# Later turns for streamed modulation sums, a later place for the gate sigmoids, and two accumulators in the first column group of a decoder layer

## The chip, the cores and the metric

The kernel runs on one core of a Trainium2 chip. The metric is the device time of one execution in microseconds; the value given for a kernel is the median of its runs. A profile shows one further execution, recorded instruction by instruction.

## What is computed

One layer of a hybrid decoder trunk, in fp32: batch 1, 256 positions, model width 2048. A vector `c` modulates both norms (adaLN); three token mixers share one input projection; a gated feed-forward part follows. Cut to what matters here:

```
mod = silu(c) @ w_ada + b_ada                       # 2048 -> 6 x 2048
shift1, scale1, gate1, shift2, scale2, gate2 = split(mod, 6)
h = rms_norm(x, norm1_gain) * (1 + scale1) + shift1  # 256 x 2048
proj = h @ w_in                                      # 2048 x 13840: q, k, v of three branches, r, gate columns
q, k of the dilated branch: rms_norm per head of 128
g = sigmoid(gate columns)                            # three branches x 2048
y = g0*(o_sb @ w_br_sb) + g1*(o_dil @ w_br_dil) + g2*(o_gla @ w_br_gla)
x = x + gate1 * (y @ w_out)
h = rms_norm(x, norm2_gain) * (1 + scale2) + shift2
x = x + gate2 * ((silu(h @ Wg) * (h @ Wu)) @ w_ffn_out)
```

## The kernel before

**Products.** Every large product keeps fp32 accuracy by splitting each operand into a high part that TensorE takes in its fast fp32 format and a low rest. A weight tile of 256 x 512 arrives in a buffer `raw` (four of them), ScalarE casts the high part `whi` (line 163), VectorE subtracts the low part `wlo` (line 164), and `mm3` issues three matmuls per row block and half of the positions (lines 171 to 173: high x high, high x low, low x high). A pair of row blocks with both halves of the positions is twelve weight matmuls. The low part frees `raw` for the next transfer; all transfers named here are issued by SyncE, in program order.

**The first projection in groups.** The modulated input H is needed transposed (channels on partitions), and shift and scale of its channels come out of `w_ada`. So that the projection need not wait for all of them, the 16 blocks of 128 channels are cut into five groups (0–2, 2–5, 5–8, 8–11, 11–16). The first four run over 16 column blocks of `w_in`, up and down in turn, and add into SBUF tiles `A`; a group's last block stays in its PSUM banks and is continued by the next group (`proj_block`, `carry`). The fifth takes its 16 blocks likewise, and after it come the blocks of `r` and the column blocks of the gates. While group g runs, the modulation columns of group g+1 are computed (`ada_group`): SyncE brings a piece of 128 rows of `w_ada` into one of six borrowed buffers (`T4`, `T5`, `OS0`–`OS2`, `OD`), VectorE multiplies it with silu(c) of those rows and adds it to an accumulator `ada` (`ada_mac`, lines 296 and 298), 16 steps to a sum; ADA_BY says by which block of the projection how many steps are issued. Then TensorE transposes the accumulator in columns of 128 (`turned_sums`, line 348), VectorE adds up along the row (line 349) and finishes shift and scale (lines 355, 358), and ScalarE and VectorE make H of the group (`make_h`, lines 466 to 473). There is one accumulator tile, so the next sum begins when the transposes of this one are done. The fifth group is summed in two pieces of two and of three channel blocks, each with shift and scale.

**The first group** has nothing to hide behind. `first_group` loads x and the pieces of `w_ada`, keeps TensorE at work with matmuls on constants (`keep_warm`, line 454; 22, 13 and 10 of them), transposes x with its norm factor (line 447; eight copies to `xT` by ScalarE, line 448), and sums 16 steps into one accumulator, the last in two halves. The column sums are single-column matmuls (`column_sum`, line 340).

**Order.** Each engine runs its instructions in a fixed order that a list scheduler decides when the program is built: by priority (`prio()` raises it by 4000, in the first group by 30000), by the tiles' readiness in its model, and by explicit edges (`tc.issue_after`). So an edit in one place can shift instructions of other parts, on all engines.

**After the groups.** The gate blocks (`gate_block`): each of the three gates has four column blocks of 512. Block 1 of each is among the 16 blocks of the groups (tiles `A13` to `A15`); block 0 is multiplied after the groups and its banks are copied as they are (line 1068). The sigmoids of these six tiles are taken in place (line 1086, tiles of 128 x 1024); the other column blocks take the sigmoid straight from the bank. In the same stretch run the norms of the dilated heads (`qk_norm`: squares on ScalarE at line 646, `rsqrt` with a logarithm and an exponential at lines 278 to 286, factors applied at line 654) and the transposes of the normed heads (`qk_turn`, line 666), the gated linear attention (lines 837 to 872), and the multiply-adds of the later modulation columns. Sigmoid, logarithm and exponential need other function tables on ScalarE; a switch is an instruction ACT_TABLE_LOAD, which stands under the line of the function that needs it.

Of the kernel before, what the change touches and what calls it, by code (L numbers as in the profile page):

```python
# [13 lines left out]
AF = mybir.ActivationFunctionType  # L14
# [64 lines left out]
def trunk(ctx: ExitStack, tc: tile.TileContext, I, out):  # L79
# [16 lines left out]
    def S(tag, shape, dtype=F32):  # L96
        return slot.tile(shape, dtype, tag=tag, name=nm(tag))
# [191 lines left out]

    w_ada = I["w_ada"]  # L290

    def ada_mac(acc, raw, k, zero=True):

        c = csil[:, k : k + 1]
        if k == 0 and zero:
            nc.vector.tensor_scalar(acc, raw, c, None, op0=ALU.mult)
        else:
            nc.vector.scalar_tensor_tensor(acc, raw, c, acc, op0=ALU.mult, op1=ALU.add)  # L298

    ADA_TAGS = ("T4", "T5", "OS0", "OS1", "OS2", "OD")  # L300

    mod1 = const.tile([P, 2, KC], F32, name="mod1")

    def ada_group(k0, k1, tags=ADA_TAGS, between=None):

        n = k1 - k0
        sh, sc = mod1[:, 0, k0:k1], mod1[:, 1, k0:k1]
        gains[GROUPS.index((k0, k1))] = (sh, sc)
        count = 0
        pieces = -(-n // 4)  # L310
        for i in range(pieces):
            a = k0 + n * i // pieces
            m = k0 + n * (i + 1) // pieces - a
            w = m * P
            acc = S("ada", [P, 2, w])
            for k in range(KC):
                with prio():
                    raw = S(tags[count % len(tags)], [P, 2, w])
                    nc.sync.dma_start(
                        raw,  # L320
                        w_ada[k * P : (k + 1) * P, : 2 * D].rearrange("p (s c) -> p s c", s=2)[:, :, a * P : a * P + w],
                    )
                    with tc.issue_after(state["macs_after"]) if "macs_after" in state else nullcontext():
                        ada_mac(acc, raw, k)
                count += 1
                if k < KC - 1:
                    yield
            if between is not None:
                between()
            with prio():  # L330
                c = slice(a - k0, a - k0 + m)
                sums = small([P, 2, m])
                for j in range(2):
                    turned_sums(sums[:, j, :], acc[:, j, :])
                finish_columns(sums[:, 0, :], sh[:, c], SEG_SHIFT1, a)
                finish_columns(sums[:, 1, :], sc[:, c], SEG_SCALE1, a, ROW_N1)
            yield

    def column_sum(ps, acc):
        return nc.tensor.matmul(ps, acc, ones[:, 0:1], start=True, stop=True)  # L340

    def turned_sums(dst, acc, behind=None):

        n = dst.shape[1]
        ps = misc_bank([P, n, P])
        for i in range(n):
            with tc.issue_after(behind) if behind is not None else nullcontext():
                nc.tensor.transpose(ps[:, i, :], acc[:, i * P : (i + 1) * P], ident)  # L348
        nc.vector.reduce_sum(dst, ps, axis=AX.X)

    def finish_columns(ps, dst, seg, k0, gain_row=None):

# [63 lines left out]
    def norm1():  # L416
# [22 lines left out]
        for t in range(NT):  # L439
            act(col(r, t), col(y, t), AF.Copy, scale=col(z, t))  # L440
            act(diag[:, t, :], ident, AF.Copy, scale=col(r, t))
        for j in range(4):
            for t in range(NT):
                ps = misc_bank([P, 4, P])
                for i in range(4):
                    xs = xin[2 * t + j // 2][:, j % 2, i * P : (i + 1) * P]
                    state["turn"] = nc.tensor.matmul(ps[:, i, :], xs, diag[:, t, :], start=True, stop=True)
                state["turned"] = nc.scalar.copy(xT[j][:, :, t * P : (t + 1) * P], ps)

    def keep_warm(n):  # L450

# [62 lines left out]
                else:  # L514
                    nc.vector.tensor_add(A[b][:, t, :], A[b][:, t, :], pss[t])  # L515

    gains = [None] * len(GROUPS)

    def h_group(g):
        k0, k1 = GROUPS[g]  # L520
        sh, sc = gains[g]
# [5 lines left out]
    def first_group():  # L527
# [21 lines left out]
        split = state["split"]  # L549
        load(range(5, KC // 2))  # L550
# [9 lines left out]
        acc = S("ada", [P, 2, w])  # L560
# [30 lines left out]
    def ada_groups():  # L591
        for a, b in GROUPS[1:]:
            yield from ada_group(a, b)

    nxt, done = ada_groups(), 0
    for g in range(LAST):
        base = ADA_BY[g - 1] if g else 0
        for n, b in enumerate(orders[g]):
            due = ADA_BY[0] * n // (GROUPED - 1) if g == 0 else base + (ADA_BY[g] - base) * (n + 1) // GROUPED
            while done < due and next(nxt, "end") != "end":  # L600
                done += 1
            if (g, n) == (0, 6):
                state.pop("casts_after", None)
                state.pop("macs_after", None)
            proj_block(g, b, early if (g, n) == (0, 0) else None, carry=n == GROUPED - 1)
        if g == LAST - 1:
            for _ in nxt:
                pass
        h_group(g + 1)

    kc = S("KC", [P, 8, P])
# [448 lines left out]
    def gate_block(n, br, steps=None):  # L1060
# [22 lines left out]
    ogT = ([], [])  # L1083
    for br in range(3):
        for n in range(2):
            nc.scalar.activation(gates[n, br], gates[n, br], AF.Sigmoid)
    for j in range(2):
        sg = S(f"T{1 + j}", [P, NT, NB])
        nc.scalar.activation(sg, rr[j], AF.Sigmoid)
# [538 lines left out]
```

## Time and profile before

| | before |
|---|---|
| median of 3 runs | 1598.54 us (1594.4 to 1601.88) |
| profiled execution | 1596.89 us |
| its span | 1595.1 us |
| mean granted TensorE clock | 0.995 |
| TensorE busy | 1570.7 us, 98% |
| VectorE busy | 1349.9 us, 85% |
| ScalarE busy | 927.9 us, 58% |
| moved by DMA | 402.27 MB, mean 252 GB/s |

The span is what the profile records, from the first instruction to the last; the time of the execution is 1.8 us more. Matmuls are pipelined: one is recorded with 0.39 us while the next starts 0.227 us after it. The granted clock is TensorE's clock as a share of full speed. A row of the timeline gives start, duration, engine, line, operation, tiles out<-in and shapes, and in brackets the idle time before it with what ended it.

### The profile page before, as it was taken

Reading aid. Unit: us, or ns where it says so; the run is one execution under the profiler, and the core shown is the slowest. Engines: PE = TensorE matmul, PEld = TensorE weight load, DVE = VectorE, ACT = ScalarE, POOL = GpSimd, SP = SyncE. Lnnn points to the kernel's source line nnn. Section 1 sums busy time; section 2 is a strip of 40 time slices with the busy share of each in tenths; the row PEclk is TensorE's granted clock in tenths of the full one; section 3 lists DMA queues with packets and bytes.
Section 4 is the critical chain, followed back from the end, with each engine's and each line's share of the span. In section 5 each row is a group of like instructions: output and inputs, shape, how many; then the busy total and the mean of one; then the engine's idle time right before and its main releaser. Section 6 shows DMA issues by size and latency. Waiting matters only on the chain.

```text
span 1595.1 us, 20403 instructions
## 1 busy us (share of the span) xinstructions
PE 1570.7 (98%) x7191; PEld 1300.4 (82%) x7191; DVE 1349.9 (85%) x1663; ACT 927.9 (58%) x1323; POOL 13.2 (1%) x24
## 2 busy tenths in 40 slices
PE   8999899999999999999999999999999999999999
PEld 6888787888887888888888888888888888888887
DVE  6798986579968887879777987999999999999986
ACT  6766666888886544444445644555555555455553
POOL 1000000000000000000000000000000000000000
PEclk9999999999999999999999999999999999999999
DMA  9899988676787799899787786556665666876664
GB/s 338 310 335 299 307 289 274 195 234 225 222 283 257 270 312 318 306 336 312 242 275 244 266 299 221 194 196 202 206 199 197 211 198 198 308 237 192 224 208 150
DMA packets 200974, 402.27 MB, mean 252 GB/s; under 512 B 13662, under 2 KB 40964, under 8 KB 200872
## 3 DMA queue, kind: packets, MB, share of 16 engines
q1 hardware_dynamic: 199608, 397.75, 74.6%
q0 software_dynamic: 1088, 3.16, 0.5%
q8 instruction: 56, 0.92, 0.2%
q14 instruction: 46, 0.38, 0.1%
q10 hardware_dynamic: 176, 0.07, 0.0%
HBM read 395.68 MB, written 5.24 MB: 251 GB/s over the span
## 4 chain that ended last, share of the span: by engine, by line
PE 85%; DVE 5%; DMA 4%; ACT 3%; issue 2%; SPq 0%; DVEq 0%; ACTq 0%
PE acc L173 20%; PE acc L172 20%; PE acc L171 20%; PE misc L172 6%; PE misc L171 6%; PE misc L173 6%; DMA OS<-w_ada 2%; DVE wlo L164 2%; ACT whi L163 1%; DVE ada L298 1%; PE misc L820 1%; DMA T<-w_ada 1%; PE misc L1137 1%; PE misc L348 0%; DVE A L515 0%
## 5 line engine op out<-in xcount | busy, mean ns | idle before, releaser
L163 ACT CAST whi<-raw 128x1024 fp32r<-128x1024 f32 (+1 forms) x344 | 333.2, 971 | 282.9 <-PE acc L173 174.8
L164 DVE TENSOR_TENSOR wlo<-raw,whi 128x1024 fp32r<-128x1024 f32 (+1 forms) x344 | 383.7, 1123 | 118.6 <-ACT whi L163 117.7
L171 PE MATMUL acc<-whi,H 128*128 128x512 f32 x1145 | 449.9, 393 | 1.2 <-ACT H L466 0.8
L172 PE MATMUL acc<-wlo,H 128*128 128x512 f32 x1145 | 448.6, 392 | 1.3 <-DVE wlo L164 1.2
L173 PE MATMUL acc<-whi,H 128*128 128x512 f32 x1145 | 448.6, 392 | 0.1
L172 PEld LDWEIGHTS acc<-wlo,H 128*128 128x128 f32 x1145 | 216.2, 189 | 46.4 <-DVE wlo L164 3.2
L171 PEld LDWEIGHTS acc<-whi,H 128*128 128x128 f32 x1145 | 216.3, 189 | 45.5 <-ACT H L466 1.4
L173 PEld LDWEIGHTS acc<-whi,H 128*128 128x128 f32 x1145 | 216.1, 189 | 44.9 <-DVE H L1228 0.5
L1357 ACT CAST whi<-raw 128x1024 fp32r<-128x1024 f32 (+1 forms) x163 | 155.2, 968 | 112.6 <-PE acc L173 37.4
L1343 DVE TENSOR_TENSOR wlo<-raw,whi 128x1024 fp32r<-128x1024 f32 (+1 forms) x163 | 178.0, 1115 | 10.0 <-ACT whi L1357 8.8
L173 PE MATMUL acc<-whi,A 128*128 128x512 f32 x234 | 91.2, 390 | 0.0
L172 PE MATMUL acc<-wlo,A 128*128 128x512 f32 x224 | 87.4, 390 | 0.5 <-DVE wlo L164 0.5
L171 PE MATMUL acc<-whi,A 128*128 128x512 f32 x224 | 87.5, 391 | 0.1
L171 PE MATMUL misc<-whi,H 128*128 128x512 f32 (+1 forms) x201 | 78.3, 389 | 0.0
L172 PE MATMUL misc<-wlo,H 128*128 128x512 f32 (+1 forms) x201 | 78.1, 388 | 0.0
L173 PE MATMUL misc<-whi,H 128*128 128x512 f32 (+1 forms) x201 | 78.0, 388 | 0.0
L513 ACT COPY A<-acc 128x512 f32<-128x512 f32 x107 | 61.8, 582 | 20.0 <-PE acc L173 18.2
L1343 DVE TENSOR_TENSOR A<-raw,A 128x1024 fp32r<-128x1024 f32 (+2 forms) x59 | 61.2, 1049 | 5.2 <-ACT A L1357 4.8
L1357 ACT CAST A<-raw 128x1024 fp32r<-128x1024 f32 (+1 forms) x47 | 46.0, 989 | 33.0 <-PE acc L173 12.3
L503 ACT COPY acc<-A 128x512 f32<-128x512 f32 x75 | 43.9, 594 | 16.8 <-DVE A L515 16.7
L173 PEld LDWEIGHTS acc<-whi,A 128*128 128x128 f32 x234 | 44.0, 188 | 9.1
L298 DVE SCALAR_TENSOR_TENSOR ada<-AR,csil,ada 128x1024 f32<-128x1024 f32 x39 | 49.5, 1281 | 2.0 <-DMA AR<-w_ada 1.9
(505 smaller groups left out, 2544.2 us busy)
## 6 DMA issues: line engine op xcount, KB each, us to landing
raw<-w_in SPq DMA_DIRECT2D x186, 512.0 KB, 4.9
raw<-w_ffn_in SPq DMA_DIRECT2D x176, 512.0 KB, 4.6
raw<-w_ffn_out SPq DMA_DIRECT2D x74, 512.0 KB, 5.3
AR<-w_ada SPq DMA_DIRECT2D x58, 512.0 KB, 5.1
raw<-w_in SPq DMA_DIRECT2D x64, 256.0 KB, 3.8
raw<-w_out SPq DMA_DIRECT2D x32, 512.0 KB, 5.4
OS<-w_ada SPq DMA_DIRECT2D x31, 384.0 KB, 5.8
KC<-w_ada SPq DMA_DIRECT2D x23, 512.0 KB, 5.5
```

Of the source, the lines that this page charges most:

```text
L163: state["cast"] = nc.scalar.copy(hi[:, :n, :], raw[:, :n, :])
L164: state["split"] = nc.vector.tensor_tensor(lo[:, :n, :], raw[:, :n, :], hi[:, :n, :].bitcast(F32), op=ALU.subtract)
L171: nc.tensor.matmul(ps, lh, rh, start=start, stop=False, skip_group_check=seeded)
L172: nc.tensor.matmul(ps, lh, rl, start=False, stop=False, skip_group_check=seeded)
L173: state["mm"] = nc.tensor.matmul(ps, ll, rh, start=False, stop=stop, skip_group_check=seeded)
L298: nc.vector.scalar_tensor_tensor(acc, raw, c, acc, op0=ALU.mult, op1=ALU.add)
L503: nc.scalar.copy(pss[t], A[b][:, t, :])
L513: nc.scalar.copy(A[b][:, t, :], pss[t])
L820: nc.tensor.matmul(ps[:n, t * N_GLA + h, :].rearrange("p (s l) -> p s l", l=L), at(f, h, t)[:, :n], odd(at(f, h, t)), start=True, stop=True,)
L1137: nc.tensor.transpose(ps[:, i, :], src[:, i * P : (i + 1) * P], ident)
L1343: done = nc.vector.tensor_tensor(dst, x, y, op=ALU.subtract)
L1357: nc.scalar.copy(hi[:, :n, :], src)
```

## The change

- **Stream of pieces.** `ada_stream` replaces `ada_group` for groups two to five. The groups of three blocks keep their pieces (shift and scale together); the fifth takes shift and scale as separate pieces of five blocks. Two accumulator tiles, `ada` and `AR0`, are used in turn. A piece's turn (`turn_piece`: transposes, row sums, finishing) is issued three steps after its last step, or ahead of the last block of the group before it is needed, behind the latest weight matmul issued by then; its row sums go out with priority.
- **Gate sigmoids.** The six sigmoids in place are ordered behind the last bank copy of column block 0 of the last gate (weight matmul 2016).
- **First group.** Even and odd steps add into two accumulators, each column sum becomes two matmuls, the last step is not halved, the weight cast of the first tile is ordered behind the fourth copy to `xT`, and the last run of constant matmuls is 6 long instead of 10.

In the order of the built programs the turns stand, counted in weight matmuls from the first: for the second group at 180 (before: 170; its H is needed at 192), for the third at 444 (382; 480), for the fourth at 660 (580; 768), for the fifth at 876 and 1038 (710 and 905; 1056). The transposes of the dilated queries stand at 1674 and 1692 (1731 to 1740).

```diff
-WARM = (22, 13, 10)
+WARM = (22, 13, 6)
...
-    def ada_mac(acc, raw, k, zero=True):
+    def ada_mac(acc, raw, k, zero=True, fresh=False):
 
         c = csil[:, k : k + 1]
-        if k == 0 and zero:
+        if k == 0 and zero or fresh:
             nc.vector.tensor_scalar(acc, raw, c, None, op0=ALU.mult)
...
+    ADA_LATE = 3
...
+    def ada_stream():
+
+        pieces = []
+        for g, (k0, k1) in enumerate(GROUPS):
+            if g and k1 - k0 <= 4:
+                pieces.append((g, (0, 1)))
+            elif g:
+                pieces += [(g, (j,)) for j in range(2)]
+        step = 0
+        for i, (g, js) in enumerate(pieces):
+            k0, k1 = GROUPS[g]
+            w = (k1 - k0) * P
+            acc = S(("ada", "AR0")[i % 2], [P, len(js), w])
+            c0 = js[0] * D + k0 * P
             for k in range(KC):
                 with prio():
+                    raw = S(ADA_TAGS[step % len(ADA_TAGS)], [P, len(js), w])
...
                     with tc.issue_after(state["macs_after"]) if "macs_after" in state else nullcontext():
                         ada_mac(acc, raw, k)
+                step += 1
+                if turns and turns[0][0] <= step:
+                    turns.pop(0)[1]()
+                if k == KC - 1:
+                    turns.append((step + ADA_LATE, lambda g=g, js=js, acc=acc, n=k1 - k0: turn_piece(g, js, acc, n)))
+                yield
+
+    def turn_piece(g, js, acc, n):
+        finish = mod_columns(g)
+        for i, j in enumerate(js):
+            sums = small([P, n])
+            half = (n + 1) // 2 if n > 4 else n
+            for a in range(0, n, half):
+                turned_sums(sums[:, a : min(n, a + half)], acc[:, i, a * P : min(n, a + half) * P], state["mm"].ins, True)
             with prio():
+                finish(j, sums)
+
+    def column_sum(ps, acc, start, stop):
+        return nc.tensor.matmul(ps, acc, ones[:, 0:1], start=start, stop=stop)
+
+    def turned_sums(dst, acc, behind=None, soon=False):
...
-        nc.vector.reduce_sum(dst, ps, axis=AX.X)
+        with prio() if soon else nullcontext():
+            nc.vector.reduce_sum(dst, ps, axis=AX.X)
...
-        state["casts_after"] = c_exp.ins
-        early.extend(load_weights(w_in, 0, n, column(orders[0][0]), ahead=False))
...
-        norm1()
+        turned = norm1()
+        state["casts_after"] = turned[3].ins
+        early.extend(load_weights(w_in, 0, n, column(orders[0][0]), ahead=False))
...
-        acc = S("ada", [P, 2, w])
-        for k in range(KC - 1):
-            with tc.issue_after(split.ins) if k >= 13 else nullcontext():
-                ada_mac(acc, raws[k], k)
+        acc = S("ada", [P, 2, 2, w])
+        for k in range(KC):
+            with tc.issue_after(split.ins) if k >= 14 else nullcontext():
+                ada_mac(acc[:, k % 2], raws[k], k, fresh=k < 2)
...
-        for q in range(n):
-            ada_mac(acc[:, :, chunk(q)], raws[KC - 1][:, :, chunk(q)], KC - 1)
...
             for j in range(2):
-                with tc.issue_after(behind.ins):
-                    behind = column_sum(sums[:, j : j + 1], acc[:, j, chunk(q)])
+                for i in range(2):
+                    with tc.issue_after(behind.ins):
+                        behind = column_sum(sums[:, j : j + 1], acc[:, i, j, chunk(q)], i == 0, i == 1)
...
+            if n == GROUPED - 1:
+                while turns and (g == LAST - 1 or turns[0][0] <= ADA_LATE + KC * (g + 1)):
+                    turns.pop(0)[1]()
             proj_block(g, b, early if (g, n) == (0, 0) else None, carry=n == GROUPED - 1)
-        if g == LAST - 1:
-            for _ in nxt:
-                pass
...
-                    nc.scalar.copy(g[:, t, :], pss[t])
+                    state["gates0"] = nc.scalar.copy(g[:, t, :], pss[t])
...
     for br in range(3):
         for n in range(2):
-            nc.scalar.activation(gates[n, br], gates[n, br], AF.Sigmoid)
+            with tc.issue_after(state["gates0"].ins):
+                nc.scalar.activation(gates[n, br], gates[n, br], AF.Sigmoid)
```

More of the change, by code (lines that the diff above doesn't have):

```diff
@@ L300, in trunk @@
     ADA_TAGS = ("T4", "T5", "OS0", "OS1", "OS2", "OD")
+    ADA_LATE = 3
     mod1 = const.tile([P, 2, KC], F32, name="mod1")
[L304 to L314, printed above, removed]
-            acc = S("ada", [P, 2, w])
+    gains = [None] * len(GROUPS)
@@ new lines, in trunk, with mod_columns, finish @@
+    turns = []
+    def mod_columns(g):
+        k0, k1 = GROUPS[g]
+        gains[g] = mod1[:, 0, k0:k1], mod1[:, 1, k0:k1]
+        def finish(j, sums):
+            finish_columns(sums, gains[g][j], (SEG_SHIFT1, SEG_SCALE1)[j], k0, ROW_N1 if j else None)
+        return finish
+    def ada_stream():
[7 more added lines that the diff above has]
+        for i, (g, js) in enumerate(pieces):
+            k0, k1 = GROUPS[g]
+            w = (k1 - k0) * P
+            acc = S(("ada", "AR0")[i % 2], [P, len(js), w])
+            c0 = js[0] * D + k0 * P
@@ L316, in ada_group @@
             for k in range(KC):
                 with prio():
[L318 to L322, printed above, removed]
+                    raw = S(ADA_TAGS[step % len(ADA_TAGS)], [P, len(js), w])
+                    rows_k = w_ada[k * P : (k + 1) * P]
+                    if len(js) == 2:
+                        nc.sync.dma_start(raw, rows_k[:, : 2 * D].rearrange("p (s c) -> p s c", s=2)[:, :, c0 : c0 + w])
+                    else:
+                        nc.sync.dma_start(raw[:, 0, :], rows_k[:, c0 : c0 + w])
@@ L323, in ada_group @@
                     with tc.issue_after(state["macs_after"]) if "macs_after" in state else nullcontext():
                         ada_mac(acc, raw, k)
[L325 to L329, printed above, removed]
-            with prio():
[L331 to L336, printed above, removed]
@@ L441, in norm1 @@
             act(diag[:, t, :], ident, AF.Copy, scale=col(r, t))
+        turned = []
         for j in range(4):
@@ L589, in trunk @@
         nc.vector.tensor_scalar(qg_sb[:, 1:2], vec[:, ROW_DILQ : ROW_DILQ + 1], rs, None, op0=ALU.mult)
[L591 to L595, printed above, removed]
+    nxt, done = ada_stream(), 0
     for g in range(LAST):
```

13 lines of the change are left out of this document (4 added, 9 removed).

## The prediction

> **What bounds the kernel now.** I read the page first, then the waits of TensorE, then the stretches round those waits, and last the queue of each engine that TensorE waited for.
>
> ```profile
> PE 1570.7 (98%) x7191; PEld 1300.4 (82%) x7191; DVE 1349.9 (85%) x1663; ACT 927.9 (58%) x1323; POOL 13.2 (1%) x24
> ```
>
> TensorE is busy for 98% of the span, and the change takes no weight matmul away (the counts of both programs are equal but for four column sums more and four warming matmuls less). So only time that TensorE loses can be won: where it stands still, and where it runs below full clock after standing still. Its waits between 100 and 500 us, where everything that the change touches after the first group lies:
>
> ```profile
> PE misc L348 <- DVE ada L298: 8.2, 3, 3.7
> PE misc L666 <- DVE A L654: 3.1, 1, 3.1
> PE acc L172 <- DVE wlo L164: 1.2, 2, 0.7
> ```
>
> Three turns of modulation sums (line 348) wait for the multiply-adds on VectorE, the turn of the dilated queries (line 666) waits once, and a low weight half comes late twice. In the windows (time, TensorE, its weight loads, VectorE, ScalarE, GpSimd, granted clock, DMA share, GB/s) the waits are followed by a lower clock:
>
> ```profile
> 180.00:200.00 20.00, 17.44 (x76) 14.15 (x75) 17.62 (x26) 11.39 (x17) 0.00 (x0) 0.95 0.94 304
> 200.00:220.00 20.00, 20.00 (x86) 16.43 (x86) 16.15 (x25) 12.91 (x21) 0.00 (x0) 0.96 0.88 291
> 240.00:260.00 20.00, 16.29 (x69) 13.22 (x68) 14.50 (x22) 11.21 (x20) 0.00 (x0) 0.91 0.84 276
> 480.00:500.00 20.00, 16.89 (x82) 14.30 (x81) 16.82 (x37) 11.03 (x24) 0.00 (x0) 0.83 0.77 263
> 580.00:600.00 20.00, 20.00 (x90) 16.58 (x89) 14.60 (x14) 8.47 (x10) 0.00 (x0) 1.00 0.92 319
> 130.00:250.00 120.00, 110.49 (x480) 89.61 (x479) 101.89 (x137) 71.59 (x110) 0.00 (x0) 0.98 0.90 297
> ```
>
> Undisturbed, the clock is 1.00 (580 to 600). Behind the second turn the missing share costs 20 × (0.05 + 0.04) = 1.8 us, behind the third 20 × 0.09 = 1.8, behind the dilated turn 20 × 0.17 = 3.4. So at stake are 8.2 + 1.2 + 3.6 = **13.0 us** in the stretch of the modulation pieces, and 3.1 + 3.4 = **6.5 us** at the dilated turn.
>
> The unit for shifts in the program is one weight matmul; twelve of them (one pair of row blocks) take 2.72 us, 0.227 each:
>
> ```profile
> 70.16 0.39 PE L171 MATMUL acc<-whi,H 128*128 128x512 f32 x1
> ...
> 72.88 0.39 PE L171 MATMUL acc<-whi,H 128*128 128x512 f32 x1
> ```
>
> **First group: −1.1 us (0 to −1.6).** TensorE and VectorE ahead of the first projection:
>
> ```profile
> 20.69 3.84 PE L447 MATMUL misc<-H,A 128*128 128x128 f32 x32 [1.36 <-ACT T L448]
> 24.28 2.57 PE L454 MATMUL acc<-H,ones_r 128*128 128x512 f32 x10
> 26.69 0.95 PE L340 MATMUL misc<-ones_r,ada 128*128 128x1 f32 x8
> 28.39 0.50 PE L171 MATMUL acc<-whi,H 128*128 128x512 f32 x1 [0.75 <-ACT H L466]
> ```
> ```profile
> 11.81 7.06 DVE L298 SCALAR_TENSOR_TENSOR ada<-A,csil,ada 128x512 f32<-128x512 f32 x9 [0.28 <-DMA A<-w_ada]
> 19.93 0.75 DVE L298 SCALAR_TENSOR_TENSOR ada<-A,csil,ada 128x512 f32<-128x512 f32 x1 [1.05 <-DMA A<-w_ada]
> 20.60 1.22 DVE L164 TENSOR_TENSOR wlo<-raw,whi 128x1024 fp32r<-128x1024 f32 x1
> 21.73 4.03 DVE L298 SCALAR_TENSOR_TENSOR ada<-A,csil,ada 128x512 f32<-128x512 f32 x6
> ```
>
> The sums start at 26.69, behind ten warming matmuls of 0.24 each (26.69 − 24.28, over 10), though VectorE was done at 21.73 + 4.03 = 25.76. The change leaves six warming matmuls (−1.0 us) and moves the first weight cast on ScalarE behind the fourth copy of x, so part of the 1.36 us wait for those copies goes too. Multiply-adds on two accumulators do not read what the one before wrote. A dependent one takes 7.06 / 9 = 0.78 us from start to start; an independent next operation followed after 20.60 − 19.93 = 0.67. Five after 20.60, with the 1.13 us of the weight half among them, end near 20.60 + 1.13 + 5 × 0.67 = 25.1, or 25.3 with a little lateness of data. Four sums instead of two ahead of the first H add 0.95 / 4 = 0.24. So 25.3 + 0.24 − 26.69 = −1.1. The weight half is due at 28.4 only and has the room. In the worst case TensorE's warming was what set the clock at the start, and nothing is left.
>
> The Trainium skill ("VectorE: DVE Perf Modes", section "The DRAIN you can't avoid") says that each VectorE operation flushes the pipe before the next and that a semaphore between them costs nothing extra, by which the second accumulator would bring nothing and the sum would stand about 0.5 us higher; the two spacings quoted here, 0.78 and 0.67, speak against that.
>
> **Boundary into the second group: +1.5 us (0 to +2.5).** Its turn moves from weight matmul 170 to 180, and its H is needed at 192.
>
> ```profile
> 67.19 0.82 PE L348 MATMUL misc<-ident,ada 128*128 128x128 f32 x6
> ...
> 71.88 0.60 ACT L466 ACTIVATE H<-T,mod 128x256 fp32r<-128x256 f32 x1
> ```
>
> From the first transpose to the end of H takes 72.48 − 67.19 = 5.3 us. The cover was 0.57 of transposes (67.19 to the next weight matmul at 67.76) and 22 × 0.227 = 5.0; it is now 0.57 + 12 × 0.227 = 3.3. That leaves 2.0 uncovered; the reduce now goes out with priority, so I take 1.5. The turns of the third (382 to 444, needed at 480) and fourth group (580 to 660, needed at 768) keep 8 us and more of cover. The last group's two pieces turn at 876 and 1038, needed at 1056: 18 × 0.227 = 4.1 us against 5.3, with the banks of a whole group still to be copied out; I cost it at 0, up to +2.
>
> **Pieces of groups two to four: −9 us (−3 to −13).** TensorE arrives at each turn three steps after the last multiply-add instead of at once. That takes the waits of line 348 away as such, but not their source. VectorE's own waits from 130 to 250, and the landing time of a piece:
>
> ```profile
> DVE ada L298 <- DMA OS<-w_ada: 6.8, 4, 2.4
> DVE ada L298 <- DMA T<-w_ada: 6.6, 5, 2.2
> DVE ada L298 <- DMA OD<-w_ada: 2.2, 2, 1.5
> DVE wlo L164 <- ACT whi L163: 1.4, 2, 0.8
> DVE tiny L349 <- PE misc L348: 0.8, 1, 0.8
> ```
> ```profile
> OS<-w_ada SPq DMA_DIRECT2D x31, 384.0 KB, 5.8
> ```
>
> Busy 101.9 + 15.6 on transfers + 1.4 + 0.8 = 119.7 of 120 us: VectorE is full, and round it runs a loop. SyncE's queue puts a piece's transfer behind a weight tile's, which waits until VectorE has made the low half of an older tile; the piece lands 5.8 us later and VectorE waits for it, ahead of the next low half. TensorE takes those low halves almost at once (two waits of line 172), so what VectorE loses TensorE loses later. TensorE alone would need 120 − 13 = 107 us. The later turn takes out the two small waits (2.2: no reduce stands behind a fresh transpose, no cast behind a stopped TensorE). The last group's steps change only in size (640 columns each, where they were 512 and 768); the 80 steps and their bytes stay, and in SyncE's queue a piece's transfer shifts by a transfer or two at most. Of the 48 multiply-adds of these groups 21 stand only two weight tiles behind the release that starts their transfer, and 17 after: 15.6 × 4 / 21 = 3.0 less. That is −5.2 for sure if the rest stays; −13 if the three stops of TensorE also made the transfers late, since a stopped TensorE frees no weight tile. I take the middle, −9. The bound on the small side is −3: the transfer part alone.
>
> **Dilated turn and sigmoids: −6.5 us (0 to −6.5, or a loss: see the third rival).** The four query transposes move up from weight matmul 1731–1740 to 1674 and 1692: TensorE asks 57 × 0.227 = 12.9 us earlier and was 3.1 early before, so the chain ahead of it must shrink by 16.0. That chain runs over ScalarE's queue, from 415 to 482 us:
>
> ```profile
> L1086 ACT ACT_TABLE_LOAD x3 | 3.8, 1283 | 0.1
> L1086 ACT ACTIVATE A<-A 128x1024 f32<-128x1024 f32 x3 | 3.2, 1061 | 0.0
> L871 ACT ACTIVATE scr<-misc 128x256 f32<-128x256 f32 x8 | 3.1, 390 | 4.2 <-PE misc L869 4.2
> L837 ACT ACT_TABLE_LOAD x2 | 2.6, 1283 | 0.0
> L280 ACT ACT_TABLE_LOAD x2 | 2.6, 1283 | 0.0
> L281 ACT ACT_TABLE_LOAD x2 | 2.6, 1283 | 0.0
> ```
> ```profile
> 477.73 0.18 DVE L283 TENSOR_TENSOR tiny<-tiny 128x24 f32<-128x24 f32 x1 [0.87 <-ACT tiny L281]
> ...
> 485.15 2.56 DVE L654 TENSOR_TENSOR A<-A,tiny 128x256 f32<-128x256 f32 x5
> ```
>
> With the sigmoids of line 1086 gone from among the norms' functions, the program has twelve table loads fewer in all. Nine in this stretch are 9 × 1.283 = 11.5 us, three sigmoids 3.2: 14.7. On VectorE, lines 283 to 286 lay spread over 477.73 to 485.15, with four multiply-adds and two low halves between; now they follow each other, which frees some 5 us. Together 19.7 against 16.0: cover of 3.7 us. What comes next late is the dilated scores (1742 to 1710), behind the same cover. The six sigmoids now run behind column block 0 of the last gate (weight matmul 2016): 6 × 1.061 + one load of 1.283 = 7.6 us in one run on ScalarE. Behind them queue casts of weight tiles and bank copies; ScalarE is busy for 58%, and this lies far ahead of the gate products. I cost it at 0; without that cover it is the 7.6.
>
> The Trainium skill ("ScalarE: Activation LUTs", section "What ACT_TABLE_LOAD costs") puts a switch at 1283 ns and a drain of 1380 ns behind it; the 1283 agrees with the rows, and by the page the relief would be twice as large, with no other sum.
>
> **Sum.** −1.1 + 1.5 − 9 + 0 − 6.5 = −15.1. The profiled execution took 1596.89 us (span 1595.1): 1581.8. The median, 1598.54, lies 1.65 above it: **1583.4 us**.
>
> **Rivals.** 1: *the loop over VectorE, SyncE's queue and the transfers stays the bound*; TensorE waits for low halves (line 172) where it waited for turns, and only 3 of 9 us come. For it: 119.7 of 120 full. Against it: the waits stood at turns, not at low halves. 1589.4.
> 2: *the dilated turn waits as before*, since one of its 16 us fails (a norm's table load stays, a copy of a late column block sets it): 6.5 us less gained, 1589.9.
> 3, on the other side: *the earlier query turn is not met.* If ScalarE's queue gains nothing ahead of line 281, because column block copies and weight casts set it and not the loads, TensorE reaches the transposes 57 matmuls earlier and stands for 3.1 + 12.9 us. With a relief r the term is 16.0 − r of wait + 3.4 of clock − 6.5; below r = 4.3 it eats the 8.6 that the other terms give, and from there the change loses. At r = 0 it is +12.9 in place of −6.5: 1583.4 + 19.4 = 1602.8, and 1608.8 with the first rival. Against it: lines 1086, 837, 280 and 281 have no idle time before them.
> 4: *the change moves waits only*: what the turns lose comes back at group boundaries, no net gain, 1598.
>
> **Chances.** Forecast 0.52, first rival 0.17, second 0.13, third 0.11, fourth 0.07. The forecast's own terms reach from 1576 to 1592. The range 1575 to 1599 takes in rivals one, two and four and leaves out the third and a tail. About 0.5% (8.0 us) is what a measurement can tell here: faster means under 1590.5, slower over 1606.5. Faster: the forecast (0.50) and a little over half of rivals one and two (0.16): 0.66. Slower: the part of the third rival that meets the first, with other mishaps: 0.08. Same: 0.26.
>
> **What would show it.** In the changed profile: no wait of the turn's transposes for multiply-adds; waits for low halves under 4 us between 130 and 250, or the first rival is right; clock 1.00 from 180 to 260; some 1.5 us of wait for H at the second group's start; four table loads in the program instead of sixteen; no wait at the dilated query turn, near 470 us. The prediction is wrong if TensorE's busy share does not rise by about 1%, or if a new wait longer than 4 us stands at the dilated turn or among the gate blocks.

## The result, and the profile after

The changed kernel takes 1587.98 us (median of 5 runs, 1583.76 to 1588.48), the kernel before 1598.79 in the same series: a ratio of 0.9928, with a 95% interval of 0.9907 to 0.9950. The forecast of 1583.4 lay 4.6 us under it. The profiled execution of the changed kernel took 1587.98 us (span 1586.2), 8.9 less than that of before, where the sum had said 15.1.

The page's first row, and TensorE's waits between 100 and 500 us:

```profile
PE 1567.8 (99%) x7195; PEld 1294.5 (82%) x7195; DVE 1349.3 (85%) x1659; ACT 912.6 (58%) x1311; POOL 12.7 (1%) x24
```
```profile
PE acc L172 <- DVE wlo L164: 3.1, 7, 0.6
PE acc L173 <- DVE H L494: 1.4, 1, 1.4
PE misc L756 <- ACT A L681: 0.4, 1, 0.4
```

ScalarE has twelve instructions fewer, the table loads. The waits of the turns (8.2 us) and of the dilated queries (3.1) are gone; seven short ones for low halves are there instead of two, and one for the low part of H. Four of the prediction's windows, and ahead of them one at the start:

```profile
20.00:40.00 20.00, 18.41 (x93) 15.23 (x93) 17.06 (x29) 12.47 (x18) 0.00 (x0) 0.91 1.06 375
180.00:200.00 20.00, 18.84 (x83) 14.56 (x82) 18.53 (x27) 14.56 (x24) 0.00 (x0) 1.00 0.91 302
200.00:220.00 20.00, 19.54 (x86) 15.84 (x85) 16.63 (x24) 11.07 (x16) 0.00 (x0) 1.00 0.93 298
240.00:260.00 20.00, 20.00 (x92) 16.66 (x91) 16.21 (x22) 12.90 (x20) 0.00 (x0) 1.00 0.94 312
480.00:500.00 20.00, 20.00 (x96) 16.68 (x95) 17.79 (x52) 12.99 (x35) 0.00 (x0) 1.00 0.84 272
```

The clock is 1.00 behind the turns and 0.91 at the start, where the kernel before has 1.00:

```profile
20.00:40.00 20.00, 18.56 (x101) 15.78 (x102) 18.11 (x31) 14.54 (x24) 0.00 (x0) 1.00 1.06 373
```

TensorE's timeline of the changed kernel shows what lies ahead of the low clock:

```profile
22.52 1.64 PE L475 MATMUL acc<-H,ones_r 128*128 128x512 f32 x6
24.75 0.35 PE L358 MATMUL misc<-ones_r,ada 128*128 128x1 f32 x2 [0.59 <-DVE ada L298]
25.80 1.72 PE L358 MATMUL misc<-ones_r,ada 128*128 128x1 f32 x14 [0.70 <-DVE ada L298]
27.83 0.50 PE L171 MATMUL acc<-whi,H 128*128 128x512 f32 x1 [0.31 <-ACT H L487]
...
29.45 0.63 PE L171 MATMUL acc<-whi,H 128*128 128x512 f32 x1
29.88 0.63 PE L172 MATMUL acc<-wlo,H 128*128 128x512 f32 x1
```

The six warming matmuls end at 24.16; TensorE then stands twice for VectorE, with single-column matmuls between, and from 29.45 on a weight matmul starts every 0.43 us instead of 0.23 until 32.8.

**Where the 8.9 us lie.** VectorE's low weight halves come in the same sequence in both programs, so the start of the n-th one, counted from 0, serves as a milestone (it runs one to four microseconds ahead of TensorE, and the lead varies by about as much). The table gives the milestone in the kernel before and, for the changed kernel and all experiments, by how many us later (+) or earlier (−) it is, each from one profile:

| | first matmul | 5 (start) | 30 | 48 | 120 | 150 | 200 | 380 |
|---|---|---|---|---|---|---|---|---|
| before, at us | 28.4 | 38.6 | 98.1 | 137.0 | 299.1 | 394.2 | 561.7 | 1098.3 |
| changed | −0.6 | +1.0 | +2.2 | +2.0 | −3.5 | −3.4 | −9.6 | −9.0 |
| only_sig | 0.0 | 0.0 | +1.1 | +2.2 | −1.4 | −1.4 | −7.6 | −6.6 |
| only_stream | +0.5 | +0.5 | +4.2 | +6.9 | −2.9 | −3.0 | −4.1 | −5.3 |
| only_first | −0.7 | −0.7 | +1.7 | −0.8 | +2.5 | +2.9 | +1.0 | +2.0 |
| warm10 | −0.4 | +1.1 | +7.0 | +9.5 | +1.3 | +1.1 | −5.1 | −3.8 |
| warm8 | −0.8 | +2.0 | +8.0 | +10.8 | +8.5 | +8.3 | +2.1 | +6.9 |
| warm9 | −0.9 | +0.7 | +2.2 | +1.3 | −6.1 | −6.2 | −12.4 | −12.2 |
| late0 | −0.6 | +0.9 | +2.3 | +2.0 | −5.1 | −5.1 | −11.3 | −11.1 |
| turn_now | −0.6 | +0.9 | +4.0 | +1.4 | +1.3 | +1.3 | −4.9 | −4.0 |
| one_room | −0.6 | +1.0 | +2.1 | +4.2 | −2.1 | −2.3 | −8.5 | −7.7 |
| lead2 | −1.0 | +3.4 | +3.0 | +3.4 | −7.5 | −7.3 | −13.5 | −11.6 |
| no_transfer | −1.0 | +1.7 | +16.7 | +15.3 | +3.3 | +3.7 | −2.5 | −0.3 |
| best10 | +0.1 | +2.7 | +2.4 | +1.6 | −4.9 | −4.8 | −11.0 | −9.6 |

In lead2 and best10 milestone 5 stands behind two multiply-adds more; TensorE itself is only 0.9 and 0.7 us late there.

Groups two to four run from milestone 16 to 111, the dilated turn lies between 150 and 200. For the changed kernel: start +1.0; boundary into the second group +1.2 (to 30); pieces −5.7 (30 to 120); dilated turn −6.2 (150 to 200); the rest +0.7.

### The profile page after: what moved, and what is told of

Same layout as the page of the kernel before. It is cut to its first block, busy times and chain, and to the rows that moved or that the text cites. A ratio compares the mean times of both kernels' runs of the same rounds, so it can differ in the third digit from the quotient of the medians.

```text
span 1586.2 us, 20406 instructions
## 1 busy us (share of the span) xinstructions
PE 1567.8 (99%) x7195; PEld 1294.5 (82%) x7195; DVE 1349.3 (85%) x1659; ACT 912.6 (58%) x1311; POOL 12.7 (1%) x24
## 4 chain that ended last, share of the span: by engine, by line
PE 82%; DMA 7%; DVE 5%; ACT 3%; issue 1%; SPq 0%; DVEq 0%; ACTq 0%
PE acc L173 20%; PE acc L172 20%; PE acc L171 20%; PE misc L173 6%; PE misc L171 6%; PE misc L172 6%; DMA raw<-w_in 3%; DVE wlo L164 2%; DMA OS<-w_ada 1%; DMA A<-w_ada 1%; ACT whi L163 1%; PE misc L834 1%; DMA T<-w_ada 1%; PE misc L1152 1%; DMA raw<-w_br_sb 0%
## 5 line engine op out<-in xcount | busy, mean ns | idle before, releaser
L534 ACT COPY A<-acc 128x512 f32<-128x512 f32 x107 | 62.1, 583 | 16.7 <-PE acc L173 15.3
L1372 ACT CAST A<-raw 128x1024 fp32r<-128x1024 f32 (+1 forms) x47 | 45.9, 988 | 33.8 <-PE acc L173 12.4
```

Of the source, the lines that this page charges most:

```text
L534: nc.scalar.copy(A[b][:, t, :], pss[t])
L1372: nc.scalar.copy(hi[:, :n, :], src)
```

## The experiments

Theory: four parts that add up, as the prediction summed them. The rival that the runs brought up: the parts share VectorE's queue, whose order the scheduler lays anew with every edit. A ratio is to the kernel before in the same series.

### The sigmoids alone (only_sig)

```diff
-                    nc.scalar.copy(g[:, t, :], pss[t])
+                    state["gates0"] = nc.scalar.copy(g[:, t, :], pss[t])
...
-            nc.scalar.activation(gates[n, br], gates[n, br], AF.Sigmoid)
+            with tc.issue_after(state["gates0"].ins):
+                nc.scalar.activation(gates[n, br], gates[n, br], AF.Sigmoid)
```

> The kernel before with the order of the six gate sigmoids alone changed. Theory: the table loads and sigmoids ahead of the dilated norm are all that the query turn waited for, so the 3.1 us wait and the low clock from 480 to 500 us go although the turn stands 57 weight matmuls earlier, and the time falls by 6.2 us whatever the modulation pieces do: 1592.5, no wait of line 666. Rival: VectorE's relief by the later modulation turns was needed too; then a wait of 2 to 6 us stays at the turn and the time falls by under 3 us.

Measured: 0.9969 (0.9957 to 0.9981), −5.0 us; 1591.95 against 1596.71. TensorE's waits from 100 to 500 us are the turns' and the low halves', with none at the dilated turn:

```profile
PE misc L348 <- DVE ada L298: 7.9, 4, 3.1
PE acc L172 <- DVE wlo L164: 1.3, 4, 0.5
```

The step from milestone 150 to 200 is −6.2. It is −6.2 in each of the eleven kernels in which the sigmoids are moved, whatever the rest does, and −1.1 and −1.9 in the two in which they are not. So this part stands by itself, and VectorE's relief by the stream is not needed for it. Against those two kernels, though, it is worth 4.3 to 5.1 us. They wait 3.1 us at the dilated turn like the kernel before, but the clock behind the wait is 1.00 in both, where the kernel before has 0.83; in only_stream:

```profile
480.00:500.00 20.00, 16.28 (x90) 13.47 (x91) 17.85 (x41) 13.33 (x32) 0.00 (x0) 1.00 0.77 257
```

So the wait is there in each profile without the new order, and the 3.4 us of low clock behind it are not.

### The stream alone, the first group alone, and ten warming matmuls

The first takes the changed kernel without the sigmoids' order and with the old first group, the second the kernel before with the new first group. The third is one number:

```diff
-WARM = (22, 13, 6)
+WARM = (22, 13, 10)
```

> The kernel before with the stream of pieces, the later turns and the two accumulators alone. Theory: +1.35 us at the second group's start (wait for H) and -5.7 from there to the fifth group: -4.3, 1594.4; TensorE waits for low halves 3 us in all between 130 and 250, the dilated turn still waits 3 us. Rival: part of what the trace shows belongs to the other edits through a shifted start; then under 2 us or over 7 us.

Measured: 0.9989 (0.9978 to 1.0000), −1.8 us where −4.3 was expected: under the 2 us that the rival had given.

> The kernel before with the first-group edits alone: two accumulators, later weight cast, six warming matmuls. Theory: the first weight matmul starts 0.5 us earlier, but TensorE stands still twice before the sums and then runs under full clock for 3 to 4 us, so the first group ends 1.0 us later: 1599.8, granted clock about 0.91 from 20 to 40 us. Rival: the low clock in the changed kernel comes from elsewhere; then clock 1.00 and 0.5 us faster, 1598.3.

Measured: 1.0013 (1.0003 to 1.0023), +2.1 us. The size is near the expected one, but not the way there: the clock from 20 to 40 us is 1.00, the start is 0.7 earlier at milestone 5, and the loss comes later, between 48 and 120, in code that this edit does not touch.

> The changed kernel with ten warming matmuls in the last run again instead of six. Theory: TensorE stands still for less than 0.5 us before the sums, the low clock from 28 to 33 us goes, first weight matmul about where it is (27.8 to 28.2): 1.2 to 1.6 us faster than the changed kernel, about 1586.5, clock 1.00 from 20 to 40 us. Rival: the sums move behind the longer warming by 1 us and nothing is gained: 1587.5 to 1588.5.

Measured: 0.9976 (0.9965 to 0.9988), 1593.03 us: neither of the two. It is some 8 us short of the changed kernel's gain, and the low clock at the start (0.91) stays.

The three parts alone give −5.0 − 1.8 + 2.1 = −4.7 us by their series (some 3 us either way, by their intervals), all together −11.5 (0.0072 of 1598.79; −8.0 to −14.9). So they do not add in the series. In the profiled executions they nearly do: 1590.61, 1592.91 and 1599.08 us against 1596.89 are −6.3 − 4.0 + 2.2 = −8.1, where the changed kernel has −8.9. That the whole is more than its parts is thus not settled; that one edit does not cost the same beside another is seen in single stretches. In the table, only_stream and warm10 lose 6.4 and 8.4 us between milestones 5 and 48, where the changed kernel loses 1.0: at the start of the second group and in it.

### Where the turn stands and how many accumulators (late0, turn_now, one_room)

```diff
-    ADA_LATE = 3
+    ADA_LATE = 0
```

> The changed kernel with the turns issued right after a piece's last step (third group at weight matmul 408 instead of 444, fourth at 642 instead of 660, first piece of the fifth at 858 instead of 876; the others where they are). Theory 1, the lateness is what hides the waits: the turns wait again, 2 us each with half clock behind, 4 to 8 us slower than the changed kernel. Theory 2, the loop over VectorE, the queue and the transfers sets the pace and the place of the turn only decides where TensorE waits: within 1.5 us of the changed kernel, more wait at turns and less for low halves.

Measured: 0.9938 (0.9926 to 0.9951), 1587.21 us: in time as the second theory has it, but not in its waits, for TensorE waits at no turn, and for low halves 3.0 us in six. The three steps of lateness are worth nothing measurable.

```diff
-    ADA_LATE = 3
+    ADA_LATE = 0
...
-                turned_sums(..., state["mm"].ins, True)
+              with prio():
+                turned_sums(..., None, True)
```

> The changed kernel with the turns where the kernel before had them (weight matmuls 174, 382, 587, 748 and 910: no lateness and no order behind the latest weight matmul), two accumulators and the other pieces kept. Theory: TensorE then waits at the turns again, two to four times for 2 to 3 us with low clock behind, 4 to 6 us slower than the changed kernel: 1592 to 1594. Rival: with two accumulators VectorE keeps up and the place of the turns is without meaning: 1587 to 1589, no wait of the transposes.

Measured: 0.9978 (0.9967 to 0.9990), 1593.9 us, by the ratios 6.4 us above late0, and the waits of the turns are back:

```profile
PE misc L367 <- DVE ada L298: 5.3, 2, 3.1
PE misc L367 <- DVE AR L298: 4.3, 2, 3.4
```

late0 and turn_now have the same lateness of zero steps. turn_now leaves out the order of the transposes behind the latest weight matmul and raises their priority, and its last four turns stand at weight matmuls 382, 587, 748 and 910, where late0 has 408, 642, 858 and 1038. TensorE waits at these four (0.9, 3.1, 3.4 and 2.1 us), and the low clock of turn_now (0.98 from 120 to 300 us) goes with its waits. So the turns' place does matter over these 26 to 128 weight matmuls (5.9 to 29 us); the 36, 18 and 18 more that three steps add at three of the turns do not. (Each of the two also has an order of its own on VectorE, of which more below.)

```diff
-            acc = S(("ada", "AR0")[i % 2], [P, len(js), w])
+            acc = S("ada", [P, len(js), w])
```

> The changed kernel with one accumulator for all pieces, turns at the same places. Theory: the next piece's first multiply-add must wait for the late transposes, VectorE stands with everything behind it (low halves too) for three steps' worth, so the low halves come late at each of four turns: 8 to 20 us slower than the changed kernel. Rival: the scheduler puts the multiply-adds behind and catches up: under 3 us slower.

Measured: 0.9946 (0.9932 to 0.9959), 1588.98 us: in time as the rival has it. By the ratios that is 2.9 us above the changed kernel, and the two intervals overlap, so the second accumulator is worth little; what VectorE did in its place was not read from the trace.

### What holds VectorE up (lead2, no_transfer)

In lead2 the loop body is split: `fetch(s + 2)` issues the transfer two steps on, the multiply-add of step s follows.

```diff
+    ADA_LEAD = 2
...
+                for f in range(s, min(len(steps), s + ADA_LEAD + 1)):
+                    if f not in raws:
+                        fetch(f)
+                    ada_mac(acc, raws[s], k)
```

> The changed kernel with each piece's transfer issued two steps ahead of its multiply-add (the ring of six buffers allows it). If the wait of VectorE for transfers is what makes the low halves late, those waits (some 16 us between 75 and 300 us) shrink to under 4 us, TensorE's waits for low halves (3.1 us) go, and the time falls by 3 to 5 us: about 1584. If VectorE's own work sets it, nothing moves by more than 1 us.

Measured: 0.9935 (0.9923 to 0.9948), 1586.41 us. In the stretch of the pieces its profile gains more than the changed kernel's: −10.5 us from milestone 30 to 120 instead of −5.7, and TensorE's waits for low halves from 75 to 300 us are 0.7 us in two, against 3.1 in seven. But VectorE's waits for pieces in this stretch fell from 16.0 us to 12.4 only, not to under 4, and programs without the lead also gain more than 5.7 us there (late0 7.4, warm9 8.3), so the gain is not shown to come from the lead. At milestone 380 its profile is 2.6 us ahead of the changed kernel's. The series do not show that much: their ratios, 0.9935 and 0.9928, are the same within their intervals.

```diff
-                    raw = S(ADA_TAGS[step % len(ADA_TAGS)], [P, len(js), w])
+                    if step < len(ADA_TAGS):
+                        raw = S(ADA_TAGS[step % len(ADA_TAGS)], [P, len(js), w])
+                        kept.append(raw)
+                    else:
+                        raw = kept[step % len(ADA_TAGS)]     # no transfer
```

> The changed kernel without the transfers of the pieces of groups two to five after the first six: the multiply-adds read the six pieces that lie there, so the sums are those of other numbers. If the transfers' landing is what holds VectorE up, TensorE waits nowhere between 80 and 290 us and the time falls by 4 to 6 us, 1582 to 1584: the bound of what any earlier issue can bring. If VectorE's work or the weight tiles' transfers hold it up, 3 us of wait for low halves stay, 1586 to 1588.

Measured: 0.9978 (0.9969 to 0.9987), 1594.46 us, slower than the changed kernel. Its stretches have to be read one by one. The window from 95 to 290 us:

```profile
95.00:290.00 195.00, 195.00 (x871) 161.14 (x870) 150.75 (x199) 131.33 (x200) 1.80 (x1) 1.00 0.67 200
```

TensorE waits nowhere here, at full clock. From milestone 30 to 120 the kernel gains 16.7 − 3.3 = 13.4 us, about the 13.0 that the prediction had put at stake: so much TensorE does lose there. To what it loses it, this kernel does not tell by itself. VectorE is busy for 150.75 of 195 us, but not with all of its work. Its multiply-adds of line 298 in the window (VectorE's time, count, clock, DMA share, GB/s), first without the transfers, then in the changed kernel:

```profile
95.00:290.00 195.00, 30.38 (x34) 1.00 0.67 200
95.00:290.00 195.00, 49.76 (x53) 1.00 0.92 301
```

Nineteen of them had run before the window. With their 19.4 us in it, VectorE would be busy for some 170 of 195 us (87%), by an estimate from these rows, so there would be room; but no run shows TensorE without waits and all multiply-adds in place. The weight tiles of `w_in` also landed sooner (512 KB in 4.3 us instead of 4.8). That the transfers of the pieces are the bound, and not VectorE's own work, is therefore argued from its waits and this estimate, and not shown. What the kernel lost, it lost earlier, most of it in one stop of 10.79 us, for which VectorE's timeline (rows between left out) gives the reason:

```profile
77.16 0.61 DVE L296 TENSOR_SCALAR ada<-OS,csil 128x768 f32<-128x768 f32 x1
77.69 1.01 DVE L298 SCALAR_TENSOR_TENSOR AR<-OS,csil,AR 128x768 f32<-128x768 f32 x1
...
87.91 1.01 DVE L298 SCALAR_TENSOR_TENSOR ada<-OS,csil,ada 128x768 f32<-128x768 f32 x1
88.84 0.41 DVE L502 TENSOR_TENSOR H<-scr,H 128x256 fp32r<-128x256 f32 x1
```

With no transfers to wait for, the scheduler put a dozen multiply-adds in front of the first low part of H, and TensorE stood still behind them.

### The order of VectorE's queue (warm8, warm9)

If that is also what made warm10 slow, the time must follow the order and not the number of warming matmuls. In the programs with 6 and 9 of them the first low part of the second group's H stands on VectorE behind 18 low weight halves, with 8 and 10 behind 20.

```diff
-WARM = (22, 13, 6)
+WARM = (22, 13, 8)      # and 9
```

> The changed kernel with eight warming matmuls in the last run. In its program, as with ten, all three low parts of H of the second group stand on VectorE behind 20 low weight halves; with six and with nine the first stands behind 18. Theory: this order of VectorE's queue, not the warming, made the run with ten slow; then 1592 to 1594 here, with waits for H and for low halves from 70 to 145 us and tile 48's low half 5 us or more later than in the changed kernel. Rival: the length of the warming decides; then about 1590.5, halfway between six and ten.

> The changed kernel with nine warming matmuls, whose program has the order of six at the second group's start. Theory, the order decides: 1587 to 1589, as with six, and faster than with eight. Rival, the length decides: 1591 to 1592.5, slower than with eight.

Measured: 0.9998 (0.9986 to 1.0010), 1596.52 us, with eight, and 0.9920 (0.9905 to 0.9935), 1585.35 us, with nine. One warming matmul of 0.24 us more makes the kernel 11 us faster. With 6, 8, 9 and 10 the ratios are 0.9928, 0.9998, 0.9920 and 0.9976: the length does not decide. The order had been named before these two runs, and the times went with it, by more than either expectation gave. VectorE's timeline at the second group's start, first with eight, then with nine:

```profile
76.80 1.83 DVE L164 TENSOR_TENSOR wlo<-raw,whi 128x1024 fp32r<-128x1024 f32 x2 [0.68 <-ACT whi L163]
78.54 1.01 DVE L298 SCALAR_TENSOR_TENSOR AR<-T,csil,AR 128x768 f32<-128x768 f32 x1
79.47 1.09 DVE L494 TENSOR_TENSOR H<-scr,H 128x256 fp32r<-128x256 f32 x3
```
```profile
74.65 0.42 DVE L494 TENSOR_TENSOR H<-scr,H 128x256 fp32r<-128x256 f32 x1
75.31 1.83 DVE L164 TENSOR_TENSOR wlo<-raw,whi 128x1024 fp32r<-128x1024 f32 x2 [0.24 <-ACT whi L163]
77.05 1.01 DVE L298 SCALAR_TENSOR_TENSOR AR<-T,csil,AR 128x768 f32<-128x768 f32 x1
77.98 0.75 DVE L494 TENSOR_TENSOR H<-scr,H 128x256 fp32r<-128x256 f32 x2
```

With eight, two low halves and a multiply-add go ahead of the first low part of H, which starts 4.8 us later; 1.3 of that the kernel was late by already at milestone 5, after a slower start (clock 0.83 from 20 to 40 us, with nine 0.91). TensorE's waits for low halves and for H up to 300 us, with eight and then with nine:

```profile
PE acc L172 <- DVE wlo L164: 5.7, 9, 1.2
PE acc L173 <- DVE H L494: 3.5, 2, 2.4
```
```profile
PE acc L172 <- DVE wlo L164: 2.7, 5, 1.1
PE acc L173 <- DVE H L494: 1.1, 1, 1.1
```

The other kernels bear this out. Of those with the stream, only_stream and warm10 too have 20 low halves ahead of that low part, and with warm8 they are the three that stand at +6.9 us or more at milestone 48 (no_transfer has 20 as well, and its long stop). The seven with 18 stand at +1.3 to +4.2. VectorE's waits for pieces from 75 to 300 us go the same way: 23.5 us with eight, 15.0 with nine.

The two orders differ in more places than this one (dozens of VectorE instructions stand elsewhere), and the loss goes on through the group: the first low part of H is the first difference, and that it alone costs the whole is not shown. The profiled run with eight, 1603.83 us, is also its slowest; of its +6.9 us at milestone 380 I use only the sign.

### Transfers ahead with the old first group (best10)

lead2 with the first group of the kernel before.

> The changed kernel with each piece's transfer issued two steps ahead and the first group of the kernel before (one accumulator, ten warming matmuls, early weight cast). Theory: the stretch of the pieces costs about 2 us instead of 7 (from 2.3 behind the kernel before to 8.6 ahead of it, as in the run with the transfers ahead), the start loses no clock: 1 us faster than that run, 1585. Rival: the first group's order on VectorE shifts what follows and the gain of the earlier transfers is lost: 1588 or more.

Measured: 0.9923 (0.9910 to 0.9936), 1585.99 us. The clock from 20 to 40 us is 1.00, but from milestone 30 to 120 it gains 7.3 us, where lead2 gains 10.5. It is as fast as the changed kernel within the interval (0.9928) and as warm9 (0.9920); no run beats the changed kernel clearly.

## Why the prediction was right, and where it was off

**The bound** was read rightly: only time that TensorE loses could be won. Busy share 98% to 99%, weight matmuls unchanged.

**First group, −1.1, measured +1.0.** This is the step that failed in sign. Two of its terms were wrong. The last multiply-add was to end at 25.3; it ended as before:

```profile
19.80 3.00 DVE L298 SCALAR_TENSOR_TENSOR ada<-A,csil,ada 128x512 f32<-128x512 f32 x4 [1.38 <-DMA A<-w_ada]
22.72 1.22 DVE L164 TENSOR_TENSOR wlo<-raw,whi 128x1024 fp32r<-128x1024 f32 x1
23.86 0.74 DVE L298 SCALAR_TENSOR_TENSOR ada<-A,csil,ada 128x512 f32<-128x512 f32 x1
24.99 0.75 DVE L298 SCALAR_TENSOR_TENSOR ada<-A,csil,ada 128x512 f32<-128x512 f32 x1 [0.39 <-DMA A<-w_ada]
```

24.99 + 0.75 = 25.74, against 25.76: the last piece's landing sets it, not VectorE. And I let the clock at the start stand; the 1.6 us between first matmul (−0.6) and milestone 5 (+1.0) are the low clock, eight weight matmuls that take 0.2 us more each. On alternating accumulators the multiply-adds before the weight half stand 3.00 / 4 = 0.75 apart, not 0.67: most of the expected gain by independence did not come, so the rule of the Trainium skill ("VectorE: DVE Perf Modes", section "The DRAIN you can't avoid") was nearer to it than my row, though 0.79 before, which is (7.06 − 0.75) / 8, and 0.75 after are not equal. The 0.67 is the distance from a multiply-add to the subtraction of a weight half, and stands there again (19.80 + 3 × 0.75 = 22.05, then 22.72). The clause "in the worst case TensorE's warming was what set the clock" named the danger and bounded it at zero instead of below.

**Boundary into the second group, +1.5: measured +1.2.** TensorE's timeline shows the two waits:

```profile
74.89 0.50 PE L171 MATMUL acc<-whi,H 128*128 128x512 f32 x1 [0.86 <-ACT H L487]
...
77.34 0.51 PE L171 MATMUL acc<-whi,H 128*128 128x512 f32 x1 [0.29 <-ACT H L487]
```

**Pieces, −9 (−3 to −13): measured −5.7.** The stake was right: without the transfers the stretch gains 13.4 us, and the changed kernel gained somewhat under half of it. That VectorE's loop over SyncE's queue and the landing of transfers holds the rest fits its waits below, and was not isolated. The mis-sized term is the middle between −5.2 and −13, which no row stood for. The "−5.2 for sure" comes near in size, but by luck in its pieces: 3.0 us of waits for transfers and 2.2 of small waits were to go, and 0.8 and 1.7 went. The first rival is thus true in part: VectorE's waits for pieces from 130 to 250 us fell from 15.6 to 14.8 us only, those for the cast and the reduce from 2.2 to 0.5, and TensorE waits for low halves 3.1 us, under the 4 that I gave as the mark. Rows of VectorE's waits after:

```profile
DVE ada L298 <- DMA T<-w_ada: 5.0, 4, 1.5
DVE AR L298 <- DMA OS<-w_ada: 3.4, 2, 2.6
DVE AR L296 <- DMA T<-w_ada: 2.1, 1, 2.1
DVE ada L298 <- DMA OS<-w_ada: 1.9, 2, 1.4
DVE AR L298 <- DMA T<-w_ada: 1.5, 2, 0.8
...
DVE ada L298 <- DMA OD<-w_ada: 0.9, 1, 0.9
DVE wlo L164 <- ACT whi L163: 0.5, 2, 0.3
```

I gave the credit to the three steps of lateness, which late0 shows to be idle; the order behind the latest weight matmul, a side remark in the change, is what takes the waits off the turns (turn_now, which also raised the transposes' priority).

**Dilated turn, −6.5: measured −6.2,** and only_sig shows the part by itself. The 3.4 us of low clock in it stood in the profile of the kernel before and not behind the same wait in only_stream and only_first; measured against those, the part is 4.3 to 5.1. The relief needed was 16.0 us, worked out as 19.7; the factors of the norm now start here:

```profile
461.33 0.76 DVE L668 TENSOR_TENSOR A<-A,tiny 128x256 f32<-128x256 f32 x2
```

That is 485.15 − 461.33 = 23.8 us earlier; 3.4 of it the kernel is ahead by then (milestone 150), which leaves 20.4. That the six sigmoids cost 0 at their new place is not shown: between milestones 200 and 380 the eleven kernels that have them there lose 0.2 us (late0, warm9) to 2.2, and warm8 4.8, while of the two others only_first loses 1.0 and only_stream gains 1.2. The changed kernel loses 0.6; its TensorE waits 1.2 us for low halves from 545 to 665 us, against 0.5 in the kernel before. The third rival, a loss by the earlier query turn, did not occur. On table loads the row of 1.283 us sufficed. With the drain of 1.380 us that the Trainium skill ("ScalarE: Activation LUTs", section "What ACT_TABLE_LOAD costs") adds to each switch, the relief would have been, by an estimate, 9 × 1.38 = 12.4 us larger than the 19.7, and 20.4 was found. (The prediction's "twice as large" holds for the loads alone.)

**What was not in it at all:** the order that the scheduler lays VectorE's queue in is a term of its own, of 11 us between two neighbouring settings (warm8 against warm9), larger than any part of the sum. The prediction's sum has no row that would tell these settings apart: it would have been nearly the same for eight and ten warming matmuls, which measured 1596.52 and 1593.03 us. That the built program had the faster order was luck. The median's 10.8 us (1598.79 to 1587.98) are 72% of the forecast's 15.1.

## What to carry to other kernels

Where a scheduler orders the queues from a model of time, an edit of a quarter of a microsecond far ahead can be worth more than the change under test: compare neighbouring settings of something harmless before crediting a part, and look which short, urgent instruction (here the low part of H) stands behind work that could wait. When an engine seems full because it waits for transfers in a loop, a kernel without the transfers shows what the stretch can gain at most; but such a kernel can reorder itself, so count how much work is left in the stretch before reading its busy time. A term taken as the middle between two far ends has no row behind it: state the pieces that have one, and what the rest would need.

## What was not expected of the hardware

TensorE dropped to a matmul every 0.43 us for some 3.4 us (6 us in warm8 and no_transfer) behind the first group's column sums in most kernels with doubled sums (clock 0.91 from 20 to 40 us in the changed kernel, warm9, warm10, late0, turn_now, lead2 and one_room, 0.83 in warm8 and no_transfer), and in none with the old sums (1.00 in the kernel before, only_sig, only_stream and best10). Ten warming matmuls did not prevent it, though TensorE stood still for one short wait of 0.5 us only. But only_first, with the same doubled sums and two stops, kept 1.00. Each of these is one profile of one execution. What tells only_first from the others was not tried and is open.
